# A two-layer decoder trunk on one core: half chunks of expert weights in a pinned order, and weights loaded as 8 KB runs

## The chip, the cores and the metric

The kernel runs on one core of a Trainium2 chip. The metric is the device time of one execution in microseconds; three runs of the kernel before took 2459.33, 2452.49 and 2456.84 us, median 2456.84. Engines are called PE (TensorE, with PEld for its weight loads), DVE (VectorE), ACT (ScalarE), POOL (GpSimd) and SP (SyncE). Each works through its own queue of instructions in order.

## The reference, cut to what matters

Two layers over 1024 tokens of width 1024, float32. Layer 0 mixes tokens with a convolution module, layer 1 with a gated linear recurrence (HGRN2); after each comes a mixture of experts, and at the end a norm. The change touches only the mixture of experts:

```python
def hier_moe(h, grp_w, grp_b, exp_w, exp_b, w_gate, w_up, w_down):
    ...
    gate = (grp_val * jax.nn.softmax(top_val, axis=-1)).reshape(-1)
    expert = (grp_idx * EXPERTS_PER_GROUP + top_idx).reshape(-1)
    ...
    def expert_block(args):
        xb, e = args
        return (jax.nn.silu(xb @ w_gate[e]) * (xb @ w_up[e])) @ w_down[e]

    y = lax.map(expert_block, (x_pad.reshape(n_blocks, MOE_BLOCK, D), block_expert)).reshape(n_rows, D)
    y = (y.astype(jnp.float32) * gate_pad[:, None]).astype(h.dtype)
    return jnp.zeros((T, D), h.dtype).at[tok_pad].add(y).reshape(B, S, D)
```

There are 32 experts with w_gate and w_up of 1024 x 512 and w_down of 512 x 1024; each token goes to two experts, and a block holds 128 rows of one expert.

## The kernel before

**The loop.** `moe(l, ...)` computes one block for each expert (32), and in layer 0 one more from a list of blocks beyond an expert's first 128 rows: 33 blocks in layer 0, 32 in layer 1 (a block of layer 1's list runs only where one is needed, behind the loop). A block's rows are gathered from HBM (`gather`, an indirect DMA on POOL, line 622, into `xg`), transposed on PE (`x_T`, 8 transposes of 128x128 into the PSUM tile `tp`, line 277) and written as two parts, `xh` by ACT (line 235) and `xl`, the rest, by DVE (line 236). Every float32 product is taken as three products of such parts: `xh wh`, `xh wl`, `xl wh`.

**The weights.** An expert's weights come in six chunks of 1 MB: two of gate, two of up, two of down, called `g0 g1 u0 u1 d0 d1` here. Each is a tile `wraw` of 128 partitions x 2048 words (`load_w`, one DMA on SP's queue, line 119). `moe_src` puts contraction row k * 128 + p on partition p, so that a chunk of gate or up has four runs of 2 KB per partition, and one of down two of 4 KB. `split` cuts a chunk into two halves of 128x1024 and makes `wh` (ACT, line 223) and `wl` (DVE, line 224) of each; four buffers (`WB`) hold each kind. Six products of 128x512 use one half: gate into `pg` and up into `pu` (lines 647 to 649), down into `pd` (lines 671 to 673). So a block has 12 halves, 72 products, and 8 + 4 transposes, four of them of the hidden rows `hh`.

**Behind the products.** ACT makes silu of `pg` (line 654), DVE multiplies it by `pu` into `hh` (line 655), PE transposes it (line 277), ACT and DVE write `hth` and `htl` (lines 235, 236), and the down products follow. ACT scales `pd` by the gate into `y` (line 677), and POOL scatters `y` to HBM (line 627).

**What sets the order.** The code writes for each block i: the gather for block i + 1, g0, the transposes of h of block i - 1, g1, x_T of block i + 1, u0, u1, silu and product, then d0 and d1 of block i - 1 and its y. That is only a start: a scheduler with a model of times places the instructions on each engine, so the order on an engine differs from block to block and from layer to layer. The loads have slots in a fixed turn: 14 chunks of layer 0 and 10 of layer 1 fit on chip, and are on their way before the loop begins; SP issues the next load when DVE has read the slot's last half. `PGB` = 1 gives one buffer each for `pg` and `pu` and two for `pd`.

**Two smaller parts** run inside the first blocks: `gate_table` (line 560 on) gives each row its gate, and `list_rest` and `entry` make the list of further blocks, on DVE and POOL above all, with small products on PE.

Of the kernel before, what the change touches and what calls it, by code (L numbers as in the profile page):

```python
# [7 lines left out]
F32 = mybir.dt.float32  # L8
# [36 lines left out]
EARLY = 3        # row tiles of h that are read back before the first MoE ends  # L45
# [34 lines left out]
CONV_DVE = (1, 2)   # the vector engine  # L80
CONV_PE = (4, 5, 6, 7)    # products
# [3 lines left out]
def trunk(ctx, tc, x, conv_norm_w, conv_pw1_w, conv_pw1_b, conv_dw_w, conv_dw_b, conv_ln_g, conv_ln_b,  # L85
# [29 lines left out]
    def load_w(ap3, pool=None):  # L115
        t = (pool or ring).tile([P, WIDE if pool is wides[0] else 2048], F32, name="wraw")[:, :2048]
        a, b = ap3.shape[1], ap3.shape[2]
        v = t.rearrange("p (a b) -> p a b", a=a)
        nc.sync.dma_start(v, ap3)
        return t  # L120
# [63 lines left out]
    def mixer_consts(t1, t2, t3, t4, lp):  # L184
        """what the recurrence needs of shapes and of its bounds; t1 and t2 hold 3 * 128, t3 and t4 224 words a row."""
# [6 lines left out]
        # softmax over the two layers, its cumulative sum less the first: the second one's share  # L192
# [23 lines left out]

    def split(pool, raw):
        """a chunk of weights, by halves, as its float32r part and what that leaves."""
        for i in range(2):
            hi = pool.tile([P, 1024], F32R, name="wh", bufs=WB)  # L220
            lo = pool.tile([P, 1024], F32R, name="wl", bufs=WB)
            r = raw[:, i * 1024:(i + 1) * 1024]
            nc.scalar.activation(hi, r, AF.Copy)  # L223
            nc.vector.tensor_tensor(lo, r, hi, op=OP.subtract)  # L224
            yield hi, lo
# [12 lines left out]
    def rsqrt_small(pool, v, n):  # L238
        """1/sqrt(v) for a few columns, on the vector engine alone: Newton steps, the scale left to the end."""
# [15 lines left out]
    def norm(pool, src, wbc, dst=None, scale=False):  # L255
        """rms norm of a [128, D] tile of rows."""
# [16 lines left out]
    def transpose_n(pp, src, c0, n=4, tag="tp"):  # L273
        """n [128,128] blocks of src from column block c0 on, transposed into one bank."""
        t = pp.tile([P, 512], F32, name=tag, **({"bufs": 2} if tag == "sc" else {}))
        for a in range(n):
            turned[0] = nc.tensor.transpose(t[:, a * P:(a + 1) * P], src[:, (c0 + a) * P:(c0 + a + 1) * P], ident)  # L277
        return t

    def rows_T(pp, src, hi, lo, cs, nb=KD, tag="tp"):  # L280
        """rows src [128, nb * 128] -> hi/lo [128, nb, cs] with columns on partitions."""
        for b in range(0, nb, 4):
            n = min(4, nb - b)
            t = transpose_n(pp, src, b, n, tag)[:, :n * P].rearrange("p (a c) -> p a c", a=n)
# [23 lines left out]
    def tail_b(pool, pp, router, l, j, res, r):  # L308
        """logits of a tile from its rows: the gain of the norm lies in the weights, its scale comes last."""
# [20 lines left out]
    def route(pool, router, i0, i1, ps):  # L330
        """the experts of the rows of tiles i0 to i1 - 1, their places among the experts' rows and what goes to these."""
# [8 lines left out]
        def first_max(v, w, mx, oh):  # L340
            """oh: one-hot of the first of the largest of v [P, n, w]; mx its value."""
# [25 lines left out]
        # rank: rows before it with the same expert, in these tiles and in the tiles done  # L367
# [9 lines left out]
        # the row of y that a place goes to less 8192, in two parts  # L377
# [20 lines left out]
        if i1 == NT:  # L398
# [3 lines left out]
            # empty places: 8192 + p, out of bounds  # L402
# [3 lines left out]
        else:  # L406
            # counts of up to 8 in each row
# [37 lines left out]
    def moe_blocks(l):  # L445
        """blocks in the order in which they are computed; NE is the first one of the list."""
        if not KEEPL[l]:
            return list(range(NE + LISTED[l]))
        return list(range(NE - 1)) + [NE] * LISTED[l] + [NE - 1]

    def moe_chunks(l):
        """(expert, part) in the order in which they are used."""
        seq, prev = [], None
        blocks = moe_blocks(l)
        for e in blocks:
# [22 lines left out]
    def moe(l, router, raws, slots, after, last=None):  # L478
        """all experts of a layer; slots are the pools of its weight chunks, in turn; after is called before the end.
        Where the last block's rows stay on chip, last is called with them in two parts."""  # L480
        with ExitStack() as held:
# [258 lines left out]
            for i, e in enumerate(blocks[:nb - (KEEPL[l])] + [None]):  # L740
# [10 lines left out]
                if i:  # L751
                    ht = h_T2(hs.pop(i - 1))
# [822 lines left out]
```

## Time and profile before

| | us |
|---|---|
| runs | 2459.33, 2452.49, 2456.84 (median 2456.84) |
| span of the profiled execution | 2454.5 |
| expert loop of layer 0, from its first gate product to the stretch's end | 478 to 1115 |
| expert loop of layer 1 | 1798 to 2409 |
| PE busy in these two | 608.20 of 637.00, 584.79 of 611.00 |
| granted clock in these two | 0.98, 0.99 |

The profiled execution is one run of the same program; its span lies between the fastest run and the median. In rows of the timeline, the bracket behind an instruction is the time for which its engine had stood idle before it, and what released it. An instruction's length on PE includes its way through the array: 128x512 products stand in the trace with 0.39 us each, while the next begins earlier. "x4" behind a row joins four equal instructions in a row.

### The profile page before, as it was taken

Reading aid. Unit: us, or ns where it says so; the run is one execution under the profiler, and the core shown is the slowest. Engines: PE = TensorE matmul, PEld = TensorE weight load, DVE = VectorE, ACT = ScalarE, POOL = GpSimd, SP = SyncE. Lnnn points to the kernel's source line nnn. Section 1 sums busy time; section 2 is a strip of 40 time slices with the busy share of each in tenths; the row PEclk is TensorE's granted clock in tenths of the full one; section 3 lists DMA queues with packets and bytes.
Section 4 is the critical chain, followed back from the end, with each engine's and each line's share of the span. In section 5 each row is a group of like instructions: output and inputs, shape, how many; then the busy total and the mean of one; then the engine's idle time right before and its main releaser. Section 6 shows DMA issues by size and latency. Waiting matters only on the chain. (4 is left out here: it accounts for less than half of the span.)

```text
span 2454.5 us, 31862 instructions
## 1 busy us (share of the span) xinstructions
PE 2237.0 (91%) x11755; PEld 1845.3 (75%) x11755; DVE 1861.1 (76%) x2525; ACT 1461.1 (60%) x2034; POOL 518.3 (21%) x331
## 2 busy tenths in 40 slices
PE   7998889699999989994799999989979999999997
PEld 6777767588887767773799999977758877777774
DVE  5999656599988778885377666673489988888887
ACT  5553145488887777784334334332358877777774
POOL 1998511311110111101100000020041111111103
PEclk9998989899999999996899999989989999999999
DMA  5111133699999999977402020106269999999985
GB/s 171 59 61 58 56 138 133 219 329 372 366 378 347 345 334 345 359 248 195 152 21 68 28 78 27 61 31 221 94 224 366 380 359 353 354 358 355 350 295 237
DMA packets 252857, 547.66 MB, mean 223 GB/s; under 512 B 27313, under 2 KB 60281, under 8 KB 252696
## 3 DMA queue, kind: packets, MB, share of 16 engines
q1 hardware_dynamic: 231412, 504.22, 58.7%
q0 software_dynamic: 18720, 33.60, 3.7%
q10 hardware_dynamic: 2564, 7.75, 0.9%
q8 instruction: 94, 1.54, 0.3%
q14 instruction: 67, 0.55, 0.1%
HBM read 519.66 MB, written 60.42 MB: 236 GB/s over the span
## 5 line engine op out<-in xcount | busy, mean ns | idle before, releaser
L224 DVE TENSOR_TENSOR wl<-wraw,wh 128x1024 fp32r<-128x1024 f32 x780 | 921.3, 1224 | 121.7 <-ACT wh L223 116.0
L223 ACT ACTIVATE wh<-wraw 128x1024 fp32r<-128x1024 f32 x780 | 795.8, 1059 | 126.3 <-PE pg L649 55.7
L647 PE MATMUL pg<-wh,xh 128*128 128x512 f32 x520 | 212.9, 409 | 17.6 <-ACT xh L235 16.8
L648 PE MATMUL pg<-wl,xh 128*128 128x512 f32 x520 | 213.3, 410 | 16.4 <-DVE wl L224 16.4
L649 PE MATMUL pg<-wh,xl 128*128 128x512 f32 x520 | 209.7, 403 | 5.6 <-DVE xl L236 5.6
L648 PE MATMUL pu<-wl,xh 128*128 128x512 f32 x520 | 206.5, 397 | 2.9 <-DVE wl L224 2.8
L672 PE MATMUL pd<-wl,hth 128*128 128x512 f32 x520 | 207.1, 398 | 2.1 <-DVE wl L224 1.7
L671 PE MATMUL pd<-wh,hth 128*128 128x512 f32 x520 | 206.4, 397 | 2.6 <-ACT wh L223 1.7
L647 PE MATMUL pu<-wh,xh 128*128 128x512 f32 x520 | 204.1, 393 | 0.0
L673 PE MATMUL pd<-wh,htl 128*128 128x512 f32 x520 | 204.1, 393 | 0.0
L649 PE MATMUL pu<-wh,xl 128*128 128x512 f32 x520 | 203.3, 391 | 0.0
L622 POOL DMA_INDIRECT xg<-xD,tidx x64 | 91.5, 1429 | 523.0 <-PE tp L277 470.8
L980 POOL TENSOR_TENSOR wraw<-wraw,tap 128x1024 f32<-128x1024 f32 x60 | 173.7, 2895 | 36.0 <-ACT tap L979 31.6
L627 POOL DMA_INDIRECT yD<-y,yidx x64 | 66.1, 1033 | 543.7 <-ACT y L677 538.1
L1247 PE MATMUL pa<-wih,xh 128*128 128x256 f32 x512 | 147.3, 288 | 2.6 <-ACT q L1228 2.6
L235 ACT ACTIVATE xh<-tp 128x512 fp32r<-128x512 f32 x146 | 84.4, 595 | 108.3 <-PE tp L277 107.6
L1247 PE MATMUL pa<-wil,xh 128*128 128x256 f32 x512 | 147.3, 288 | 0.0
L1247 PE MATMUL pa<-wih,xl 128*128 128x256 f32 x512 | 147.3, 288 | 0.0
L648 PEld LDWEIGHTS pg<-wl,xh 128*128 128x128 f32 x520 | 100.4, 193 | 48.7 <-DVE wl L224 29.6
L647 PEld LDWEIGHTS pg<-wh,xh 128*128 128x128 f32 x520 | 100.5, 193 | 41.6 <-ACT xh L235 19.4
L649 PEld LDWEIGHTS pg<-wh,xl 128*128 128x128 f32 x520 | 100.4, 193 | 30.7 <-DVE xl L236 11.1
L236 DVE TENSOR_TENSOR xl<-tp,xh 128x512 fp32r<-128x512 f32 x146 | 98.0, 685 | 31.1 <-ACT xh L235 29.7
(457 smaller groups left out, 4859.5 us busy)
## 6 DMA issues: line engine op xcount, KB each, us to landing
wraw<-in_moe_w_gate_dram SPq DMA_DIRECT2D x130, 1024.0 KB, 7.7
wraw<-in_moe_w_up_dram SPq DMA_DIRECT2D x130, 1024.0 KB, 7.9
wraw<-in_moe_w_down_dram SPq DMA_DIRECT2D x130, 1024.0 KB, 7.9
wraw<-in_hgrn_w_in_dram SPq DMA_DIRECT2D x16, 1024.0 KB, 8.1
wraw<-in_conv_pw_w_dram SPq DMA_DIRECT2D x12, 1024.0 KB, 9.8
xD<-xn SPq DMA_DIRECT2D x16, 512.0 KB, 2.9
my<-yD SPq DMA_DIRECT2D x16, 512.0 KB, 12.3
wraw<-yD SPq DMA_DIRECT2D x16, 512.0 KB, 9.8
```

Of the source, the lines that this page charges most:

```text
L223: nc.scalar.activation(hi, r, AF.Copy)
L224: nc.vector.tensor_tensor(lo, r, hi, op=OP.subtract)
L236: turned[2] = nc.vector.tensor_tensor(lo, ps, hi, op=OP.subtract)
L622: return nc.gpsimd.indirect_dma_start(out=xg, out_offset=None, in_=xD[l][:, :], in_offset=bass.IndirectOffsetOnAxis(ap=idx, axis=0), bound ...
L647: nc.tensor.matmul(ps, xh[:, kk], wh[:, k], start=(kk == 0), stop=False)
L648: nc.tensor.matmul(ps, xh[:, kk], wl[:, k], start=False, stop=False)
L649: done = nc.tensor.matmul(ps, xl[:, kk], wh[:, k], start=False, stop=(kk == KD - 1))
L671: nc.tensor.matmul(pd[:, ns], hh[:, kk], wh[:, ns], start=(kk == 0), stop=False)
L672: nc.tensor.matmul(pd[:, ns], hh[:, kk], wl[:, ns], start=False, stop=False)
L673: turned[0] = nc.tensor.matmul(pd[:, ns], hl[:, kk], wh[:, ns], start=False, stop=(kk == KF - 1))
L980: nc.gpsimd.tensor_tensor(res[c], res[c], t, op=OP.add)
L1247: nc.tensor.matmul(pa[:, :256], x_[:, k, js], w_[:, k].rearrange("p z c -> p (z c)"), start=(k == 0 and w_ is wh and x_ is xh), stop=(k == ...
```

## The change

It has three parts.

**Weights in one run per partition.** `moe_src` now puts contraction row p * 8 + k (p * 4 + k for down) on partition p, and a chunk is half of that partition's contiguous words: 2048 words, 8 KB, in one run. The contraction tile k of x then holds columns k, k + 8, k + 16 and so on, so `transpose_n` gets an argument `every` and reads `xg` with a stride of 8 words and `hh` with a stride of 4.

**An order written out.** `moe_halves` lists the half chunks in the order of use: g0, g1, u0, u1 of block i, then d0, d1 of block i - 1 (for the last block of layer 1 the down halves stand behind g0). The loop runs over halves; `s_` counts them in a block, 0 to 3 gate, 4 to 7 up, 8 to 11 down. `prepare(n + LEAD)` makes `wh` and `wl` of the half that is used three later. Around each group stands `with inorder`: every instruction of PE, DVE and ACT written in it gets a dependency, without a semaphore, on the one written before it on the same engine, so the scheduler keeps the order.

**Places.** x of block i + 1 is transposed behind the second and the third up half of block i; `hh` of block i is multiplied after the first down half of block i - 1; its transposes stand behind the third gate half of block i + 1; `y` of block i - 2 is made behind the first gate half of block i. The gather for block i + 2 is issued at the first gate half of block i, one block earlier than before.

Lines of the profile move with it: wh 223 becomes 222, wl 224 becomes 223, transposes 277 become 303, xh/hth and xl/htl 235 and 236 become 259 and 260, the gate and up products 647 to 649 become 682, the down products 671 to 673 become 710 to 712, silu 654 becomes 853 here, y 677 becomes 720.

On PE in layer 0, at the end of one block and the start of the next, before (pd is the down product, tp the transposes of the new block's x, pg the new block's gate):

```order
L673 MATMUL pd<-wh,htl 128x512
L277 MATMUL tp<-ident,xg_3529 128x128 x8
L647 MATMUL pg<-wh,xh 128x512
L648 MATMUL pg<-wl,xh 128x512
L649 MATMUL pg<-wh,xl 128x512
```

On PE in layer 1, before, where the up products end; hh is the hidden block that the up products have just completed, xg the rows of the next block:

```order
L649 MATMUL pu<-wh,xl 128x512
L671 MATMUL pd<-wh,hth 128x512
L277 MATMUL tp<-ident,hh 128x128 x4
L277 MATMUL tp<-ident,xg_15499 128x128 x4
L672 MATMUL pd<-wl,hth 128x512
L673 MATMUL pd<-wh,htl 128x512
```

On PE in layer 1, after, from the end of the second up half to the fourth (layer 0 has the same sequence):

```order
L682 MATMUL pu<-wh,xl 128x512
L303 MATMUL tp<-ident,xg_15500 128x128 x4
L682 MATMUL pu<-wh,xh 128x512
L682 MATMUL pu<-wl,xh 128x512
L682 MATMUL pu<-wh,xl 128x512
L682 MATMUL pu<-wh,xh 128x512
L682 MATMUL pu<-wl,xh 128x512
L682 MATMUL pu<-wh,xl 128x512
L303 MATMUL tp<-ident,xg_15500 128x128 x4
L682 MATMUL pu<-wh,xh 128x512
```

The next block's x is now transposed between up halves in both layers, six and five halves ahead of its first gate product, and no longer beside the transposes of hh.

On ACT in layer 1, before, one block's worth (xh and hth read the transposes, hh is silu, y reads pd):

```order
L223 ACTIVATE wh<-wraw 128x1024 x4
L654 ACTIVATE hh<-pg 128x512
L223 ACTIVATE wh<-wraw 128x1024 x4
L235 ACTIVATE xh<-tp 128x512
L223 ACTIVATE wh<-wraw 128x1024 x2
L235 ACTIVATE xh<-tp 128x512
L223 ACTIVATE wh<-wraw 128x1024 x2
L235 ACTIVATE hth<-tp 128x512
L677 ACTIVATE y<-pd,gates 128x1024
```

The same place after:

```order
L720 ACTIVATE y<-pd,gates 128x1024
L222 ACTIVATE wh<-wraw 128x1024 x2
L259 ACTIVATE hth<-tp 128x512
L222 ACTIVATE wh<-wraw 128x1024 x2
L853 ACTIVATE hh<-pg 128x512
L222 ACTIVATE wh<-wraw 128x1024
L259 ACTIVATE xh<-tp 128x512
L222 ACTIVATE wh<-wraw 128x1024
L259 ACTIVATE xh<-tp 128x512
L222 ACTIVATE wh<-wraw 128x1024 x6
```

Before, the first xh stands four wh's behind silu, and the two of a block lie on both sides of two wh's; after, the first stands one wh behind silu and the second one wh further, with six wh's ahead of the next y.

The diff, cut to its core:

```diff
+LEAD = 3
...
     def load_w(ap3, pool=None):
         t = (pool or ring).tile([P, WIDE if pool is wides[0] else 2048], F32, name="wraw")[:, :2048]
-        a, b = ap3.shape[1], ap3.shape[2]
-        v = t.rearrange("p (a b) -> p a b", a=a)
+        v = t if len(ap3.shape) == 2 else t.rearrange("p (a b) -> p a b", a=ap3.shape[1])
         nc.sync.dma_start(v, ap3)
         return t
...
+    class InOrder:
...
+        def __exit__(self, *_):
+            assert nc.cur_bb is self.at
+            for i in self.at.bb.instructions[self.n:]:
+                if i.engine in (ET.PE, ET.DVE, ET.Activation):
+                    if i.engine in self.last:
+                        tc.add_manual_dep(i, self.last[i.engine], mybir.DependencyInfo(
+                            mybir.DependencyClass.NoSync, mybir.DependencyReason.DATA), reason="in order")
+                    self.last[i.engine] = i.name
...
-    def transpose_n(pp, src, c0, n=4, tag="tp"):
+    def transpose_n(pp, src, c0, n=4, tag="tp", every=None):
         t = pp.tile([P, 512], F32, name=tag, **({"bufs": 2} if tag == "sc" else {}))
+        sv = src.rearrange("p (c k) -> p k c", k=every) if every else src.rearrange("p (k c) -> p k c", c=P)
         for a in range(n):
-            turned[0] = nc.tensor.transpose(t[:, a * P:(a + 1) * P], src[:, (c0 + a) * P:(c0 + a + 1) * P], ident)
+            turned[0] = nc.tensor.transpose(t[:, a * P:(a + 1) * P], sv[:, c0 + a], ident)
         return t
...
+    def moe_halves(l):
+        n, seq = len(moe_blocks(l)), []
+        def part(i, *chunks):
+            return [(i, p_, c, z) for p_, c in chunks for z in range(2)]
+        for i in range(n):
+            d = part(i - 1, ('d', 0), ('d', 1)) if i else []
+            if KEEPL[l] and i == n - 1:
+                seq += part(i, ('g', 0)) + d + part(i, ('g', 1), ('u', 0), ('u', 1))
+            else:
+                seq += part(i, ('g', 0), ('g', 1), ('u', 0), ('u', 1)) + d
+        return seq if KEEPL[l] else seq + part(n - 1, ('d', 0), ('d', 1))
...
     def moe_src(l, e, part, c):
+        w = {'g': moe_w_gate, 'u': moe_w_up, 'd': moe_w_down}[part]
+        cs = slice(c * 2048, (c + 1) * 2048)
...
-        if part == 'd':
-            return moe_w_down[l, e].rearrange("(k p) d -> p k d", p=P)[:, 2 * c:2 * c + 2, :]
-        w = moe_w_gate if part == 'g' else moe_w_up
-        return w[l, e].rearrange("(k p) f -> p k f", p=P)[:, 4 * c:4 * c + 4, :]
+        return w[l, e].rearrange("(p k) f -> p (k f)", p=P)[:, cs]
...
+            def prepare(n):
...
+                if z == 0:
+                    raw_of[key] = get(key)
+                with inorder:
+                    ready[n] = split_half(mp, raw_of[key], z)
...
+            for n, (i, part, c, z) in enumerate(seq):
+                prepare(n + LEAD)
+                e = blocks[i]
+                s_ = ('g', 'u', 'd').index(part) * 4 + 2 * c + z
+                with inorder:
+                    if part == 'g':
...
+                        done = mm_half(pgs[i], xt[i], ready.pop(n), 4 * c + 2 * z)
...
+                if s_ == 0:
+                    if i + 2 < nb:
+                        gather(xgs[i % 2], cols(blocks[i + 2])[0])
...
+                if s_ == 0 and i > 1 and i - 2 in pds:
+                    with inorder:
+                        finish(pds.pop(i - 2), cols(blocks[i - 2])[2], cols(blocks[i - 2])[1])
...
+                if s_ == (1 if KEEPL[l] and i == nb - 1 else 2) and i:
+                    turn_h(i - 1)
+                if s_ == 4:
+                    hs[i] = mp.tile([P, FE], F32, name="hlast" if KEEPL[l] and i == nb - 1 else "hh", bufs=HB)
+                    with inorder:
+                        nc.scalar.activation(hs[i], pgs.pop(i), AF.Silu)
+                if s_ in (5, 6) and i + 1 < nb:
+                    with inorder:
+                        xt[i + 1] = x_T(xgs[(i + 1) % 2], xt.get(i + 1), s_ - 5)
+                if s_ == 8 and i + 1 in pus:
+                    gate_h(i + 1)
```

More of the change, by code (lines that the diff above doesn't have):

```diff
@@ L215, in mixer_consts, with split_half, __init__, __enter__ @@
             nc.vector.tensor_tensor(msk[b], m2, m3, op=OP.mult)
+    def split_half(pool, raw, i):
+        hi = pool.tile([P, 1024], F32R, name="wh", bufs=WB)
+        lo = pool.tile([P, 1024], F32R, name="wl", bufs=WB)
+        r = raw[:, i * 1024:(i + 1) * 1024]
+        nc.scalar.activation(hi, r, AF.Copy)
+        nc.vector.tensor_tensor(lo, r, hi, op=OP.subtract)
+        return hi, lo
     def split(pool, raw):
         for i in range(2):
[L220 to L225, printed above, removed]
+            yield split_half(pool, raw, i)
+    class InOrder:
+        def __init__(self):
+            self.last = {}
+        def __enter__(self):
+            self.at = nc.cur_bb
+            self.n = len(self.at.bb.instructions)
+        def __exit__(self, *_):
[6 more added lines that the diff above has]
+                    self.last[i.engine] = i.name
     def split2(pool, raw, name, eng):
@@ L517, in rows_of @@
                 nc.vector.tensor_copy(yi, f[:, 3])
-            with tc.issue_after(listed):
-                for key in list(order)[:1]:
-                    early[key] = list(split(mp, early[key]))
             def sum3(dst, v, n, pool):
@@ L721, in cols @@
                 return first["e"][1][:, 0:1], first["e"][2][:, 0:1], first["e"][3][:, 0:1]
-            xt, hs = {}, {}
-            gather(xgs[0], cols(0)[0])
+            xt, hs, pgs, pus, pds = {}, {}, {}, {}, {}
+            inorder = InOrder()
+            seq = moe_halves(l)
+            raw_of, ready = {}, {}
+            def prepare(n):
+                if n >= len(seq):
+                    return
+                i, part, c, z = seq[n]
+                key = (blocks[i], part, c)
+                if KEEPL[l] and i == nb - 1 and key not in order_last:
+                    for k_, at in zip([(key[0], p_, c_) for p_ in 'gud' for c_ in range(2)], LSLOT[l]):
+                        order[k_] = at
+                        order_last[k_] = early[k_] = get(k_)
+                if z == 0:
+                    raw_of[key] = get(key)
+                with inorder:
+                    ready[n] = split_half(mp, raw_of[key], z)
+            order_last = {}
+            with tc.issue_after(listed):
+                for n in range(LEAD - 1):
+                    prepare(n)
+            g0 = gather(xgs[0], cols(0)[0])
             g1 = gather(xgs[1], cols(1)[0])
-            xt[0] = x_T(xgs[0])
+            with inorder:
+                xt[0] = x_T(xgs[0])
+            prepare(LEAD - 1)
             if KEEPL[l]:
@@ new lines, in turn_h, with gate_h @@
+            def turn_h(i):
+                with inorder:
+                    hs[i] = h_T2(hs[i])
+            def gate_h(i):
+                with inorder:
+                    nc.vector.tensor_tensor(hs[i], pus.pop(i), hs[i], op=OP.mult)
+            for n, (i, part, c, z) in enumerate(seq):
[5 more added lines that the diff above has]
+                        if s_ == 0:
+                            pgs[i] = pp.tile([P, FE], F32, name="pg", bufs=PGB)
+                        done = mm_half(pgs[i], xt[i], ready.pop(n), 4 * c + 2 * z)
+                    elif part == 'u':
+                        if s_ == 4:
+                            pus[i] = pp.tile([P, FE], F32, name="pu", bufs=PGB)
+                        mm_half(pus[i], xt[i], ready.pop(n), 4 * c + 2 * z)
+                    else:
+                        if s_ == 8:
+                            pds[i] = pp.tile([P, D], F32, name="pd", bufs=3 - PGB)
+                        mm_down_half(pds[i], hs[i], ready.pop(n), 2 * c + z)
+                if s_ == 0:
+                    if i + 2 < nb:
+                        gather(xgs[i % 2], cols(blocks[i + 2])[0])
+                    if i and i - 1 in pus:
+                        gate_h(i - 1)
+                if s_ == 0 and i > 1 and i - 2 in pds:
+                    with inorder:
+                        finish(pds.pop(i - 2), cols(blocks[i - 2])[2], cols(blocks[i - 2])[1])
+                if i == 0 and s_ == 1:
+                    with tc.issue_after(g1.ins):
+                        gate_table(done.ins)
+                    rp.release()
+                    rp = apool(f"rest{l}", 1)
+                if s_ == (1 if KEEPL[l] and i == nb - 1 else 2) and i:
+                    turn_h(i - 1)
+                if s_ == 4:
+                    hs[i] = mp.tile([P, FE], F32, name="hlast" if KEEPL[l] and i == nb - 1 else "hh", bufs=HB)
+                    with inorder:
+                        nc.scalar.activation(hs[i], pgs.pop(i), AF.Silu)
+                if s_ in (5, 6) and i + 1 < nb:
+                    with inorder:
+                        xt[i + 1] = x_T(xgs[(i + 1) % 2], xt.get(i + 1), s_ - 5)
+                if s_ == 8 and i + 1 in pus:
+                    gate_h(i + 1)
+                    if i + 1 == nb - 1:
+                        last_turn = n + 2
+                if KEEPL[l] and s_ == 11 and i == nb - 2:
+                    with inorder:
+                        finish(pds.pop(i), cols(blocks[i])[2], cols(blocks[i])[1])
+                if not KEEPL[l] and s_ == 11 and i == nb - 2:
+                    turn_h(nb - 1)
+                if s_ == 11 or (i == 0 and s_ == 7):
+                    i += s_ == 11
@@ L778, in moe @@
                 e = blocks[-1]
-                keys = [(e, part, c) for part in 'gud' for c in range(2)]
-                for key, pool in zip(keys, LSLOT[l]):
-                    order[key] = pool
-                    early[key] = get(key)
-                pg = pp.tile([P, FE], F32, name="pg", bufs=PGB)
-                pu = pp.tile([P, FE], F32, name="pu", bufs=PGB)
-                for c in range(2):
-                    mm_in(pg, xt[nb - 1], get((e, 'g', c)), c)
-                for c in range(2):
-                    mm_in(pu, xt[nb - 1], get((e, 'u', c)), c)
-                hlast = h_T(pg, pu, "hlast")
+                gate_h(nb - 1)
+                hlast = hs[nb - 1]
+            else:
+                for i in (nb - 2, nb - 1):
+                    if i in pds:
+                        with inorder:
+                            finish(pds.pop(i), cols(blocks[i])[2], cols(blocks[i])[1])
             left = after()
```

92 lines of the change are left out of this document (34 added, 58 removed).

## The prediction

> **What bounds the kernel now.** I read the page's engine rows first, then busy time in stretches, then the timeline and the waits inside the slow ones. The page gives the span; the runs shown (2452.49 to 2459.33) have their median 2.3 us above it, so I sum against 2454.5 and add 2.3 at the end.
>
> ```profile
> span 2454.5 us, 31862 instructions
> PE 2237.0 (91%) x11755; PEld 1845.3 (75%) x11755; DVE 1861.1 (76%) x2525; ACT 1461.1 (60%) x2034; POOL 518.3 (21%) x331
> ```
>
> The expert loops fill 478 to 1115 us (33 blocks) and 1798 to 2409 us (32 blocks). Busy time in stretches, each cut into an early and a late part, and then two stretches inside the second loop; the columns are length, then PE, weight load, DVE, ACT, POOL with their counts, the granted clock, the DMA share and GB/s:
>
> ```profile
> 478.00:728.00 250.00, 249.12 (x1189) 201.09 (x1188) 234.94 (x316) 210.74 (x236) 50.39 (x52) 0.99 0.98 347
> 728.00:1115.00 387.00, 359.09 (x1620) 288.34 (x1618) 318.40 (x306) 293.01 (x325) 42.60 (x36) 0.98 0.91 323
> 1798.00:1979.00 181.00, 177.92 (x850) 147.00 (x849) 163.86 (x198) 147.41 (x166) 41.06 (x48) 0.98 0.95 345
> 1979.00:2409.00 430.00, 406.87 (x1833) 317.96 (x1830) 358.37 (x349) 324.48 (x371) 48.27 (x42) 1.00 0.94 338
> 1871.00:1942.00 71.00, 71.00 (x340) 59.12 (x338) 66.22 (x66) 61.61 (x69) 8.31 (x8) 1.00 1.02 378
> ```
>
> The same view of the transposes (line 277) alone:
>
> ```profile
> 728.00:1115.00 387.00, 30.98 (x223) 26.94 (x221) 0.98 0.91 323
> 1979.00:2409.00 430.00, 34.31 (x248) 28.52 (x246) 1.00 0.94 338
> 1871.00:1942.00 71.00, 6.70 (x52) 5.88 (x50) 1.00 1.02 378
> ```
>
> The early parts have a full PE (4 us idle in 431), the late parts don't. For the floor I need the pace of back-to-back work. A stretch of the timeline in layer 0 (start, length, engine, line, what, and in brackets the idle time before and its releaser), with one row of layer 1 behind it:
>
> ```profile
> 888.83 0.39 PE L672 MATMUL pd<-wl,hth 128*128 128x512 f32 x1
> ...
> 891.10 0.39 PE L673 MATMUL pd<-wh,htl 128*128 128x512 f32 x1
> ...
> 891.33 1.03 PE L277 MATMUL tp<-ident,xg 128*128 128x128 f32 x8
> 891.53 1.11 ACT L677 ACTIVATE y<-pd,gates 128x1024 f32<-128x1024 f32 x1 [0.30 <-PE pd L673]
> 892.54 1.05 ACT L223 ACTIVATE wh<-wraw 128x1024 fp32r<-128x1024 f32 x1
> ...
> 893.48 1.07 ACT L235 ACTIVATE xh<-tp 128x512 fp32r<-128x512 f32 x2
> 893.62 1.22 DVE L224 TENSOR_TENSOR wl<-wraw,wh 128x1024 fp32r<-128x1024 f32 x1 [1.14 <-ACT wh L223]
> ...
> 894.12 0.50 PE L647 MATMUL pg<-wh,xh 128*128 128x512 f32 x1 [1.76 <-ACT xh L235]
> ...
> 895.50 0.50 PE L649 MATMUL pg<-wh,xl 128*128 128x512 f32 x1 [0.64 <-DVE xl L236]
> ```
>
> ```profile
> 1888.66 0.60 PE L277 MATMUL tp<-ident,xg 128*128 128x128 f32 x4
> ```
>
> From 888.83 to 891.10 are ten products: 0.227 us each. Eight transposes take 1.03 and four 0.60, so one more costs 0.1075. A block has 72 products and 12 transposes: 72 x 0.227 + 12 x 0.1075 = **17.63 us**. Check on the stretch at 1871: 288 x 0.227 + 52 x 0.1075 = 71.0, what it took. So four blocks in a row already run at the floor, with DVE busy 66.22 and ACT 61.61 of 71: the same work fits beside PE when its order is right.
>
> The late parts against that floor: layer 0, 1397 x 0.227 + 223 x 0.1075 = 341.1 of 387, 45.9 over; layer 1, 1585 x 0.227 + 248 x 0.1075 = 386.5 of 430, 43.5 over. Together **89.4 us over 2982 / 72 = 41.4 blocks**, about 2.2 a block.
>
> What holds PE there? In layer 0 the timeline above says it: the block's own x is transposed right ahead of its gate products, and on ACT the copy of y and a wh stand ahead of xh. PE is 1.76 + 0.64 us without work and loses its overlap twice. In layer 1 it is again ACT's place in the queue:
>
> ```profile
> 2261.47 3.90 ACT L223 ACTIVATE wh<-wraw 128x1024 fp32r<-128x1024 f32 x4
> ...
> 2267.41 0.66 PE L277 MATMUL tp<-ident,hh 128*128 128x128 f32 x4 [0.56 <-DVE hh L655]
> 2267.90 0.60 PE L277 MATMUL tp<-ident,xg 128*128 128x128 f32 x4
> ...
> 2268.54 0.60 ACT L235 ACTIVATE xh<-tp 128x512 fp32r<-128x512 f32 x1 [3.17 <-PE tp L277]
> 2269.03 2.00 ACT L223 ACTIVATE wh<-wraw 128x1024 fp32r<-128x1024 f32 x2
> ```
>
> ACT stands 3.17 us at xh with four wh's done and others queued behind it; xg's transposes stand behind hh's, and those wait for DVE. The bill comes later, where PE lacks a wl. The waits of layer 1 from 2057 to 2372 (16 blocks), then one of layer 0 from 728 to 1115 (total, times, longest):
>
> ```profile
> ACT xh L235 <- PE tp L277: 53.7, 24, 3.6
> PEld pg L648 <- DVE wl L224: 18.7, 24, 1.1
> PE pg L648 <- DVE wl L224: 9.9, 16, 0.7
> ```
>
> ```profile
> PEld pg L647 <- ACT xh L235: 18.9, 9, 2.9
> ```
>
> It is not the transfers. Over 2000 to 2370 DVE waited for a load once, and over the whole span SP, which issues them, waited for slots that DVE had not yet emptied:
>
> ```profile
> DVE wl L224 <- DMA wraw<-in_moe_w_up_dram: 0.3, 1, 0.3
> ```
>
> ```profile
> SPq L119 <- DVE wl L224: 943.7, 335, 12.8
> ```
>
> **The change, part by part.** *The order.* Nothing is added on PE, ACT or DVE; instructions change places, and the ties hold each engine to its own order, without a semaphore. A half chunk is six products, 1.36 us. From gate half 0 at time 0: h's transposes stand at 4.1, the up halves begin at 5.9, x's transposes of the next block stand at 8.6 and 10.4, the down halves begin at 12.2, the next block at 17.63. So xh and xl are made 6 to 9 us before their gate products, instead of right ahead: the stalls of both layers above have no cause left. What is late next? wh for half n+3 can start when PE leaves half n-1: release 0.30 (y's row above), from wh's start to wl's 893.62 - 892.54 = 1.08, wl 1.22: 2.6 us after half n begins. PE needs that wl at 3 x 1.36 + 0.23 = 4.3. The margin of 1.7 covers the longest piece put between, y with 1.11 on ACT; behind y stand two wh's, and PE waits for those, so y is the nearest thing to a new stall, with 0.6 left. xh may stop ACT for about 0.7 us, until its transposes end, with the wh of a down half behind it: covered too. hh stands behind the wl of the last down half, so it finds pu complete; h's transposes come seven halves after pu's end. Finding PE idle there would cost what it finds now, at most 18.7 / 16 = 1.2 us a block by the row of PEld pg; the fast stretch says 0.
>
> *DVE and ACT as bounds*: 66.22 / 4 = 16.6 and 61.61 / 4 = 15.4 us a block in the fast stretch, under 17.63. DVE has 1 us to spare, no more.
>
> *The transposes read with a stride* (32 bytes in x, 16 in h). Line 1121 does the like with 8 words of stride in this trace; its weight loads (min/median/max), and four of its transposes:
>
> ```profile
> L1121 PEld LDWEIGHTS tp<-ident,wraw x32: 185/193/227, 302.3 to 418.5; 128*128 128x128 f32 x32
> ```
>
> ```profile
> 351.59 0.61 PE L1121 MATMUL tp<-ident,wraw 128*128 128x128 f32 x4
> ```
>
> Four take 0.61 against 0.60 at line 277. The weight load of a plain one is 28.52 us / 246 = 0.116 with its overlaps; if 0.193 were not hidden, 12 x (0.193 - 0.116) = 0.9 us a block. Bounds 0 and 0.9; the row of four is the nearest, so nearly nothing. I put 0.2 a block for this and the margins together: 41.4 x 0.2 = 8.3.
>
> The Trainium skill speaks against this edit: "SBUF — State Buffer", section "Door 1: The DMA port swizzle (why `[64,N]` ≈ `[32,N]`)", says that accesses pay a penalty for each new 16-byte line, so fp32 strides are free only up to 4 words. By that x's 8 transposes would pay and h's 4 not: an estimate of 8 x 0.077 x 65 = 40 us, 2412. The longer load of line 1121 agrees; its four transposes in 0.61 us say that the load stays hidden.
>
> *The loads.* The page and three stretches of DMA rows (packets, MB, share of 16 engines): 1871 to 1942, the 1 KB runs of a weight load at 1290 to 1300, and reads of y from HBM at 1120 to 1140.
>
> ```profile
> wraw<-in_moe_w_down_dram SPq DMA_DIRECT2D x130, 1024.0 KB, 7.9
> ```
>
> ```profile
> q0 software_dynamic: 18720, 33.60, 3.7%
> ```
>
> ```profile
> q1 hardware_dynamic: 10598, 25.12, 95.6%
> q0 software_dynamic: 1152, 1.66, 6.3%
> ```
>
> ```profile
> q1 hardware_dynamic: 1040, 1.05, 36.4%
> ```
>
> ```profile
> q1 hardware_dynamic: 1163, 4.27, 90.0%
> ```
>
> A block loads six chunks, 6.29 MB, and gathers and scatters 33.60 / 65 = 0.52: 6.81 MB, 18.0 us at the 378 GB/s seen. That is 0.2 to 0.4 over the pace, but by the kernel's slots 14 chunks of layer 0 and 10 of layer 1 are on chip when the loop starts (2.33 and 1.67 blocks), so transfers bind only from 33 x 17.83 / 30.7 = 19.2 us a block in layer 0 and 32 x 17.83 / 30.3 = 18.8 in layer 1. Now 8 KB runs: the mix of 2 and 4 KB took 0.956 x 16 x 71 / 10598 = 102.5 ns per 2370 B, the 1 KB runs 0.364 x 160 / 1040 = 56 ns per 1008 B. A line through both gives 301 ns for 8 KB, the mix's own rate 354 ns. With 768 packets a block on 16 engines, and 1.1 us for queue 0, that is 15.6 to 18.1 us. Under 18.8: no cost, and no gain beyond the slack, as PE never waited for a load. These are estimates; no row has 8 KB runs of weights.
>
> *Sum.* 89.4 of excess go, 8.3 come, and I keep 4 in layer 0 for its clock of 0.98 (2% of 387 is 7.7, half of it where PE stood idle anyway): 2454.5 - 89.4 + 8.3 + 4 = 2377.4, **2380 us** with the 2.3. The unknown margins alone give 2371 (none) to 2421 (1.2 a block).
>
> **The rivals.** *Each block keeps about a microsecond* (y or a strided load on PE's path, or DVE's 1 us used up by small waits): 41.4 x 1.0 in place of 8.3 gives 2413. For: DVE at 93% in the fast stretch. Against: that stretch lost nothing. Loads at 19.5 us a block (384 ns a run) come to the same: 30.7 x 19.5 - 588 = 11 and 30.3 x 19.5 - 571 = 20, so 2411. Chance 0.17.
>
> *More goes*: 637 + 611 - 65 x 17.63 = 102 lie over the floor in all, 13 outside the late parts. Without them, the 8.3 and the 4: 2454.5 - 102 + 2.3 = 2355. Chance 0.08; list and gate work on DVE remains, which speaks against.
>
> *It changes nothing*: 2457, chance 0.03, if something else than the order placed the transposes; the order rows speak against it.
>
> *Slower: 8 KB runs, one per partition at 16 KB pitch, read like y's rows.* Those rows of 4 KB lie 512 KB apart and took 0.900 x 320 / 1163 = 248 ns per 3671 B. At that rate 8 KB takes 553 ns and a block 27.6 us: 30.7 x 27.6 + 30.3 x 27.6 - 1248 = 436, so 2892. The loops become longer than today from 20.7 and 20.1 us a block, about 400 ns a run. Against: 16 KB is far from 512, and the slots' lead pays part. Chance 0.09.
>
> The Trainium skill has a rule on this ("DMA: Bandwidth & Descriptors", section "Latency and other measured facts"): a pitch of 512 KiB between partitions' rows gives 207 GB/s, larger powers of two less. The reads of y agree (4.27 MB in 20 us is 214 GB/s); no run here shows 16 KB pitch with 8 KB runs.
>
> **How the numbers follow.** The forecast has 0.63, the rivals 0.17, 0.08, 0.03 and 0.09. A measurement of this kernel tells about 0.3% from no change, 7.4 us. Faster 0.63 + 0.17 + 0.08 = 0.88, same 0.03, slower 0.09. The range runs from the case in which more goes to just past the margins' upper bound: 2355 to 2425.
>
> **What would show it.** Right: both loops at 17.6 to 18.0 us a block, PE busy over 98% in the late parts too, no row of PE behind ACT xh, ACT's wait at xh under 1 us. The loads are right if DVE has no wait for wraw and a run takes 300 to 350 ns. It is wrong if PE shows waits for wl in the half after y (margin), if four transposes take over 0.8 us (stride), if the granted clock falls where PE is full, or if DVE waits for loads from the third block on.

## The result and the profile after

The changed kernel takes **2379.34 us** (median of four runs, 2379.11 to 2380.95) against 2456.64 (2452.49 to 2459.33): a ratio of 0.9687, interval 0.9676 to 0.9699, 77 us faster. The page after, with the two groups that make the split weights:

```profile
span 2377.3 us, 31779 instructions
PE 2209.9 (93%) x11755; PEld 1856.7 (78%) x11755; DVE 1868.6 (79%) x2525; ACT 1461.4 (61%) x2034; POOL 546.4 (23%) x331
...
L223 DVE TENSOR_TENSOR wl<-wraw,wh 128x1024 fp32r<-128x1024 f32 x780 | 929.0, 1226 | 74.7 <-ACT wh L222 63.6
L222 ACT ACTIVATE wh<-wraw 128x1024 fp32r<-128x1024 f32 x780 | 805.0, 1057 | 87.6 <-PE pd L712 59.3
```

The counts are those of before, and so is the length of one instruction; what shrank is the idle time (121.7 and 126.3 before). Busy time in four stretches of the changed kernel (columns as in the prediction: length, PE, weight load, DVE, ACT, POOL, clock, DMA share, GB/s), then the transposes of line 303 alone in the second and fourth:

```profile
478.00:728.00 250.00, 248.16 (x1179) 201.79 (x1178) 237.32 (x316) 208.82 (x235) 61.01 (x49) 1.00 0.95 350
728.00:1050.00 322.00, 322.00 (x1522) 269.81 (x1521) 301.17 (x291) 273.86 (x308) 44.02 (x34) 1.00 0.98 381
1755.00:1979.00 224.00, 220.50 (x1050) 182.35 (x1050) 209.90 (x237) 186.19 (x209) 54.31 (x50) 1.00 0.96 357
1979.00:2308.00 329.00, 329.00 (x1556) 275.67 (x1555) 307.89 (x298) 279.77 (x315) 46.10 (x35) 1.00 0.98 380
```

```profile
728.00:1050.00 322.00, 33.16 (x216) 33.13 (x216) 1.00 0.98 381
1979.00:2308.00 329.00, 33.88 (x222) 33.73 (x220) 1.00 0.98 380
```

In both late parts PE is busy without a gap. At the prediction's paces (0.227 us a product, 0.1075 a transpose) the second stretch should take 1306 x 0.227 + 216 x 0.1075 = 319.7 us and took 322; the fourth 1334 x 0.227 + 222 x 0.1075 = 326.7 and took 329. So 0.13 us a block remain over the floor, where before 2.2 did. The period can be read off the transposes of h in two blocks that follow each other (timeline of PE):

```profile
911.72 0.63 PE L303 MATMUL tp<-ident,hh 128*128 128x128 f32 x4
...
929.50 0.63 PE L303 MATMUL tp<-ident,hh 128*128 128x128 f32 x4
```

That is 17.78 us, and by the first gate products blocks 11 to 31 of layer 0 and 4 to 30 of layer 1 all have it. The longest waits of DVE and of ACT (728 to 1050; total, times, longest) and ACT's order within one block:

```profile
DVE wl L223 <- ACT wh L222: 17.6, 36, 0.7
ACT xh L259 <- PE tp L303: 16.7, 36, 0.6
```

```profile
908.80 1.10 ACT L720 ACTIVATE y<-pd,gates 128x1024 f32<-128x1024 f32 x1
909.80 2.00 ACT L222 ACTIVATE wh<-wraw 128x1024 fp32r<-128x1024 f32 x2
...
916.96 0.60 ACT L259 ACTIVATE xh<-tp 128x512 fp32r<-128x512 f32 x1 [0.64 <-PE tp L303]
```

ACT still stops at xh, but 0.6 us at most, in layer 1 (1979 to 2308) too, where it was 3.6 there before. In the whole list PE appears only as what is waited for.

Where the 77 us lie, by the first gate product of a block in the two timelines (us):

| piece | before | after |
|---|---|---|
| start to layer 0's first gate product | 478.2 | 476.6 |
| layer 0, blocks 0 to 13 | 249.9 | 253.2 |
| layer 0, blocks 14 to 31 | 362.6 | 320.0 |
| layer 0's block 32 and the whole HGRN stage | 707.8 | 705.0 |
| layer 1, blocks 0 to 7 | 143.6 | 143.8 |
| layer 1, blocks 8 to 29 | 429.6 | 391.2 |
| layer 1, blocks 30 and 31, and the end | 82.7 | 87.5 |

The late blocks give 42.6 + 38.4 = 81.0. Two pieces got clearly longer: the early blocks of layer 0 by 3.3 and the end by 4.8. Two got shorter, by 1.6 and 2.8; the change barely touches them, and the first of them varies from 473.7 to 479.3 in the traces of the other runs. The end has this on ACT (the last row's idle time is the point) and this on PE:

```profile
2308.82 1.10 ACT L720 ACTIVATE y<-pd,gates 128x1024 f32<-128x1024 f32 x1
...
2313.03 1.06 ACT L222 ACTIVATE wh<-wraw 128x1024 fp32r<-128x1024 f32 x1 [3.10 <-SPq L895]
```

```profile
2314.62 0.80 PE L710 MATMUL pd<-wh,hth 128*128 128x512 f32 x1 [3.61 <-ACT hth L259]
```

### The profile page after: what moved, and what is told of

Same layout as the page of the kernel before. It is cut to its first block, busy times and chain, and to the rows that moved or that the text cites. A ratio compares the mean times of both kernels' runs of the same rounds, so it can differ in the third digit from the quotient of the medians.

```text
span 2377.3 us, 31779 instructions
## 1 busy us (share of the span) xinstructions
PE 2209.9 (93%) x11755; PEld 1856.7 (78%) x11755; DVE 1868.6 (79%) x2525; ACT 1461.4 (61%) x2034; POOL 546.4 (23%) x331
## 5 line engine op out<-in xcount | busy, mean ns | idle before, releaser
L222 ACT ACTIVATE wh<-wraw 128x1024 fp32r<-128x1024 f32 x780 | 805.0, 1057 | 87.6 <-PE pd L712 59.3
L682 PE MATMUL pu<-wh,xh 128*128 128x512 f32 x520 | 213.6, 411 | 0.0
L682 PE MATMUL pg<-wl,xh 128*128 128x512 f32 x520 | 205.0, 394 | 0.1
L682 PE MATMUL pg<-wh,xl 128*128 128x512 f32 x520 | 204.1, 392 | 0.0
L661 POOL DMA_INDIRECT yD<-y,yidx x64 | 81.7, 1277 | 519.1 <-ACT y L720 511.7
L710 PEld LDWEIGHTS pd<-wh,hth 128*128 128x128 f32 x520 | 98.6, 190 | 27.1 <-ACT hth L259 4.7
L711 PEld LDWEIGHTS pd<-wl,hth 128*128 128x128 f32 x520 | 98.4, 189 | 23.5 <-DVE wl L223 3.2
L1078 ACT ACTIVATE tap<-upl,dwT 128x1024 f32<-128x1024 f32 x60 | 68.9, 1150 | 77.5 <-POOL wraw L1079 77.5
L712 PEld LDWEIGHTS pd<-wh,htl 128*128 128x128 f32 x520 | 98.6, 190 | 21.6 <-DVE htl L260 1.3
```

The source lines that it names most:

```text
L661: s = nc.gpsimd.indirect_dma_start(out=yD[l][:, :], out_offset=bass.IndirectOffsetOnAxis(ap=idx, axis=0), in_=y, in_offset=None, bounds_ch ...
L682: done = nc.tensor.matmul(ps, x_[:, kk + k], w_[:, k], start=(kk + k == 0 and x_ is xh and w_ is wh), stop=(kk + k == KD - 1 and x_ is xl))
L710: nc.tensor.matmul(pd[:, ns], hh[:, kk], wh[:, ns], start=(kk == 0), stop=False)
L711: nc.tensor.matmul(pd[:, ns], hh[:, kk], wl[:, ns], start=False, stop=False)
L712: turned[0] = nc.tensor.matmul(pd[:, ns], hl[:, kk], wh[:, ns], start=False, stop=(kk == KF - 1))
L1078: nc.scalar.activation(t, src, AF.Copy, scale=dwT[:, c, lag:lag + 1])
```

## The experiments

All times are medians; a run with a single time is named so. The kernel before, run beside them, had 2455.0 to 2456.0.

### The two halves of the change apart

**The order alone.** The changed kernel with the old reading of the weights and plain transposes; PE, ACT and DVE keep the changed kernel's sequence.

```diff
-        return w[l, e].rearrange("(p k) f -> p (k f)", p=P)[:, cs]
+        return w[l, e].rearrange("(k p) f -> p k f", p=P)[:, 4 * c:4 * c + 4, :]
...
-                    t = transpose_n(pp, xg, 4 * b, every=KD).rearrange("p (a c) -> p a c", a=4)
+                    t = transpose_n(pp, xg, 4 * b).rearrange("p (a c) -> p a c", a=4)
```

> The pinned order with the weights loaded as before (runs of 2 and 4 KB, transposes without a stride); PE, ACT and DVE have the same instructions in the same order as the changed kernel. Theory (the order does all of it, transfers and strides cost nothing that shows): 2370 to 2380 us, a block in the middle of a loop at 17.63 to 17.78 us. Rival (the 8 KB runs are needed, because PE now asks for 6.81 MB per 17.78 us, 383 GB/s, and 2 and 4 KB runs gave 378 at most): the lead of 14 and 10 chunks is used up within a loop, DVE waits for loads towards its end, 2385 to 2420 us.

Measured: 2388.78 us (ratio to before 0.9736, 0.972 to 0.9752). Neither theory had it right. The blocks take 17.77 us to the end of both loops, as the theory says; yet it is 9.4 us slower than the changed kernel, inside the rival's range. The two profiled executions are 11.3 us apart, and 7.5 of these lie at the end (95.0 us from block 30's first gate product, where the changed kernel has 87.5): in the last block ACT waits as in the changed kernel, only longer:

```profile
2324.07 1.06 ACT L222 ACTIVATE wh<-wraw 128x1024 fp32r<-128x1024 f32 x1 [10.37 <-SPq L897]
```

**The layout alone.** The kernel before with the new `moe_src` and the strided transposes; the scheduler's sequence on PE, ACT and DVE stayed that of before.

> The scheduler's order of before with the weights loaded as 8 KB runs and the transposes read with a stride; PE, ACT and DVE have the same instructions in the same order as the kernel before. Theory (layout alone is worth nothing): within 0.3% of before, 2450 to 2464 us, PE's waits behind ACT xh and DVE wl as before. Rival (shorter transfers free slots earlier and let wh and wl run ahead): at least 10 us faster. Other rival (the strided loads cost on PE's path, 0.6 to 0.9 us a block): 2490 or more.

Measured: 2459.88 us, ratio 1.0028 (1.0018 to 1.0038): the theory. If anything it is 0.3% slower. The wait that carried the prediction is still there (2057 to 2372, 53.7 before):

```profile
ACT xh L234 <- PE tp L278: 54.1, 24, 3.7
```

**The ties.** The same written order, without the dependencies:

```diff
                 if i.engine in (ET.PE, ET.DVE, ET.Activation):
-                    if i.engine in self.last:
+                    if False:
```

> The changed kernel written in the same order, without the ties that hold PE, ACT and DVE to it: the scheduler places the instructions. Theory (it was the scheduler's order on the in-order engines that cost, and the writing alone doesn't cure it): most of the gain goes, 2420 to 2470 us. Rival (the half chunks, the longer lead of the weights and the earlier gather are the gain, ties or not): within 5 us of 2379.

Measured: 2456.47 us, ratio 1.0005 (0.999 to 1.002). The whole gain is gone: half chunks, the longer lead and the earlier gather bring nothing as long as the scheduler places the instructions. The old waits come back, in layer 1 (2050 to 2350) and in layer 0, where before had 1.76:

```profile
ACT xh L259 <- PE tp L303: 50.2, 22, 3.7
```

```profile
896.12 0.50 PE L682 MATMUL pg<-wh,xh 128*128 128x512 f32 x1 [1.75 <-ACT xh L259]
```

**Ties on ACT alone** (`if i.engine == ET.Activation`).

> The changed kernel with ties on ACT alone; the scheduler places PE's and DVE's instructions. ACT's order is nearly the changed kernel's, PE has x's transposes among the down products again. Theory (ACT's place for xh helps only if PE's transposes stand ahead of it too): ACT waits at xh for PE's transposes with wh's queued behind, most of the 77 us stays lost, 2410 to 2470 us. Rival (ACT's order alone is the cure): 2379 to 2395.

Measured, one run: 2436.8 us, so three quarters of the gain stay lost. ACT's order by itself doesn't help layer 0 (blocks 14 to 31 take 363.4 us, 362.6 before), where PE's transposes stand among the down products again and ACT waits for them (800 to 1000):

```profile
ACT xh L259 <- PE tp L303: 46.9, 10, 4.7
```

Blocks take 20.1 us there and 18.3 in layer 1. So layer 1 is another matter: the scheduler places x's transposes behind the first gate product and among the up products, ACT's wait at xh is gone from the list (2057 to 2340; 53.7 us from 2057 to 2372 before), and blocks 8 to 29 take 404.3 us, which is 25 of the 38 us gained there. Ties on PE or on DVE alone were not run.

### Which place in the order

**The lead.** `LEAD = 2`.

> The changed kernel with LEAD = 2: each wh and wl stands one half chunk (1.36 us) later in the queues of ACT and DVE. Theory (the margin at LEAD = 3 is 1.7 us, with y's 1.11 between 0.6): at 2 the wh behind y, behind hth and behind xh come too late, 0.5 to 1.5 us of PE idle a block, 2410 to 2475 us, with PE rows waiting for DVE wl. Rival (the four buffers set the lead, the place in the queue does not matter): 2379 to 2385.

Measured, one run: 2415.45 us, the theory's lower end; blocks of 18.37 us, 0.59 more. PE's weight loads wait for wl again (800 to 1000):

```profile
PEld pd L711 <- DVE wl L223: 6.5, 22, 0.4
```

That is two waits a block, at the second and the fourth down half; a third stands at the second up half (3.7 us in all, before overlap). In the block traced they come where DVE has htl, xl or hh among its wl's, and none comes in the gate halves behind y.

**x's transposes late.**

```diff
-                if s_ in (5, 6) and i + 1 < nb:
+                if s_ in (5, 6) and i == 0:
...
+                if s_ == 11 and i + 2 < nb:
+                    with inorder:
+                        xt[i + 2] = x_T(xgs[i % 2])
```

> The changed kernel with both groups of x's transposes of the next block placed behind the last down half, right ahead of the block's own gate products, where layer 0 of the kernel before had them. Everything else stays pinned. Theory (the late place of x is what stalled layer 0): PE waits for ACT xh, 0.9 us at least (release 0.3 and one xh of 0.6), up to the 2.4 us seen there, for 63 blocks: 2435 to 2530 us. Rival (the kernel before lost its time to the order of wh and wl, and x's place is nearly free): under 2400.

Measured, one run: 2426.54 us, 18.55 us a block: between the two, 0.77 a block where 0.9 was the least expected. The late place alone is not the 2.4 us that layer 0 had lost. PE's own idle time before the first gate product is 0.2 us a block (800 to 1000); the rest shows as weight loads that wait for xh and xl:

```profile
PEld pg L682 <- ACT xh L259: 4.7, 11, 0.4
PEld pg L682 <- DVE xl L260: 4.7, 11, 0.4
PE pg L682 <- ACT xh L259: 2.6, 11, 0.2
```

**And y ahead of it on ACT**: the run before with `finish` of the same block written ahead of `x_T`.

> The run with x's transposes behind the last down half (2426.5 us, 18.55 us a block), and the block's own y now ahead of xh on ACT, as layer 0 of the kernel before had it (there with a wh between, too). Theory (what ACT has ahead of xh is what makes the late place dear): y adds its 1.11 us to PE's wait, 19.4 to 20.2 us a block, 2475 to 2530 us. Rival (ACT has slack, y there costs nothing): 2420 to 2435.

Measured, one run: 2461.92 us, 19.11 us a block; below the range, but the direction is the theory's. y costs 0.56 a block, half its length, and that is what PE's idle time grows by; where the other half is covered was not traced. PE's idle time ahead of the first gate product is 0.8 us a block now (same window):

```profile
PEld pg L682 <- ACT xh L259: 10.9, 11, 1.0
...
PE pg L682 <- ACT xh L259: 8.8, 11, 0.8
```

These two places, wrong together, cost 82.6 us: a pinned order can be as slow as the scheduler's. It is not the same loss, though. The late blocks of the profiled execution take 343.9 and 420.3 us, so 53 of the 81.0 us come back there, and some 25 are lost in the early blocks of both layers, where the kernel before had lost little.

### The stride

> The changed kernel with x and hh transposed without a stride, so that rows of x and hh meet other rows of the weights than they should; loads, order and counts are those of the changed kernel. It prices the stride alone. A block of the changed kernel takes 17.78 us where 72 products and 12 transposes at the paces of before come to 17.63. If the stride is the 0.15: 17.63 a block, 65 x 0.15 = 10 us less, 2370. If the 0.15 is something else (the joints between products and transposes): 2379 as it is.

The edit is the second pair of lines of the first diff, and the like for `hh`. Measured: 2378.84 us (2377.32 to 2380.09): it is not the stride. The weight loads of x's transposes fall back from 191 to 140 ns (median) and those of hh from 205 to 139, and a block takes 17.77 us for 17.78. The changed kernel's two rows come first, then two of this run:

```profile
L303 PEld LDWEIGHTS tp<-ident,xg x520: 185/191/230, 474.8 to 2300.6; 128*128 128x128 f32 x174
L303 PEld LDWEIGHTS tp<-ident,hh x256: 197/205/212, 497.7 to 2310.6; 128*128 128x128 f32 x128
```

```profile
L303 PEld LDWEIGHTS tp<-ident,xg x520: 138/140/231, 477.5 to 2300.0; 128*128 128x128 f32 x174
L303 PEld LDWEIGHTS tp<-ident,hh x256: 138/139/144, 499.1 to 2310.0; 128*128 128x128 f32 x128
```

```profile
912.72 0.60 PE L303 MATMUL tp<-ident,hh 128*128 128x128 f32 x4
...
930.49 0.60 PE L303 MATMUL tp<-ident,hh 128*128 128x128 f32 x4
```

The joints between products and transposes remain as the explanation of the 0.15; no run takes them apart.

### The loads

**What transfers can do**, with wl left out of the expert blocks so that they are the bound; first 8 KB runs, then 2 and 4 KB.

> Transfers made the bound: the changed kernel (8 KB runs) without wl in the expert blocks, so without the third product of each three; PE has 48 products and 12 transposes a block, 12.2 us, ACT some 14.5, and the loads 6.81 MB. What the transfers can do shows in the time of a block. Theory (8 KB runs take 301 to 354 ns each, as a line through the shorter runs gave): 15.6 to 18.1 us a block once the lead is used up, 376 to 437 GB/s, with engines waiting for loads. Rival (a run of 8 KB takes 400 ns or more): over 20 us a block.

> The same without wl, with the old layout (runs of 2 and 4 KB). Theory (the mix moves 23.1 bytes per ns and engine, as in the kernel before): 17.7 to 18.3 us a block, 372 to 385 GB/s, slower than the 8 KB runs by 0 to 2.5 us a block. Rival (the layout makes no difference to what the transfers can do): the same time a block within 0.1 us.

Measured, one run each: 2296.20 and 2357.99 us. Busy time from 750 to 950, q1's packets there (q1 is the queue of the weight loads) and what ACT waits for, the 8 KB kernel first:

```profile
750.00:950.00 200.00, 161.47 (x694) 112.64 (x694) 30.09 (x45) 169.34 (x197) 23.12 (x23) 1.00 1.00 402
```

```profile
q1 hardware_dynamic: 9949, 72.45, 90.0%
```

```profile
ACT wh L787 <- DMA wraw<-in_moe_w_gate_dram: 23.1, 20, 1.4
```

```profile
750.00:950.00 200.00, 160.44 (x658) 109.37 (x659) 29.40 (x44) 162.41 (x187) 22.13 (x22) 0.97 1.02 382
```

```profile
q1 hardware_dynamic: 28857, 68.49, 91.8%
```

By the first gate products, blocks 14 to 29 of layer 0 take 17.5 and 18.3 us; both theories hold, the second at the end of its range, and both rivals fall. Per engine the 8 KB runs move 72.45 MB / (0.900 x 16 x 200 us) = 25.2 bytes per ns, the others 23.3. So the layout is worth 5% of the transfers' rate, and PE's 17.78 lies between the two: 8 KB runs keep ahead of it, 2 and 4 KB runs fall behind.

**The last loads.** `prepare` fetches all six chunks of block 31 at once, and by the program's order SP issues its d1 between g0 and d0 of block 30, and block 30's own d1 last of all, into the slot that g0 of block 31 leaves. SP's issues in the changed kernel:

```profile
2280.82 3.76 SPq L119 DMA_DIRECT2D wraw<-in_moe_w_down_dram  x2
2295.51 0.33 SPq L119 DMA_DIRECT2D wraw<-in_moe_w_gate_dram  x1
2298.60 3.75 SPq L119 DMA_DIRECT2D wraw<-in_moe_w_up_dram  x2
2305.01 3.20 SPq L119 DMA_DIRECT2D wraw<-in_moe_w_down_dram  x2
```

The second of the pair at 2305.01 is the load that ACT's wh at 2313.03 waits for. The edit, on the changed kernel and on the order with the old layout:

```diff
                         order_last[k_] = early[k_] = get(k_)
+                        if k_ == key:
+                            for dk in [(blocks[i - 1], 'd', c_) for c_ in range(2)]:
+                                raw_of[dk] = get(dk)
-                if z == 0:
+                if z == 0 and key not in raw_of:
```

> The changed kernel with one thing moved: the two down chunks of block 30 of layer 1 are issued ahead of the chunks g1, u0, u1, d0, d1 of block 31, not behind them, so that they take slots that are free earlier; the last down chunk of block 31 takes the late slot instead. In the changed kernel ACT waits 3.10 us for the last of these loads and PE stands 3.9 us. Theory (that wait is the slot's lateness): the wait goes, 3 to 4 us less, 2375 to 2377 us. Rival (the late slot only moves the wait to block 31's own down chunk, behind the branch): 2379 or a little more.

> The pinned order with the old layout of the weights (runs of 2 and 4 KB) and the same move of block 30's down chunks. There ACT waits 10.37 us for the last load of block 30, and the kernel takes 2388.8 us. Theory (transfers in 2 and 4 KB runs keep the queue full, 1.02 of its time, and run behind by the loop's end; the layout's 9 us are nearly all in this one wait): the wait goes, 2379 to 2382 us, within 5 us of the same move on the changed kernel. Rival (the old layout costs in the loops or elsewhere): 2385 or more.

Measured: **2373.13** us (2371.42 to 2375.94; ratio to before 0.9665, 0.9648 to 0.9681) and 2373.47 (2370.04 to 2375.03; 0.966, 0.9644 to 0.9676). The wait is gone; ACT's row after y in the first of them:

```profile
2307.96 1.10 ACT L720 ACTIVATE y<-pd,gates 128x1024 f32<-128x1024 f32 x1
2308.96 1.05 ACT L222 ACTIVATE wh<-wraw 128x1024 fp32r<-128x1024 f32 x1
```

The gain is 6.2 us where 3 to 4 were expected; the last stretch, 87.5 us long, now takes 82.4. PE's wait explains 2.9 of these 5.1: it was 3.61 us and is 0.69. Most of the rest is the clock: after the wait the changed kernel's products start 0.43 us apart and not 0.227, and the granted clock (third number from the end) is 0.51 over the 5.4 us that follow.

```profile
2314.60:2320.00 5.40, 5.23 (x12) 3.66 (x13) 3.28 (x4) 1.97 (x2) 0.00 (x0) 0.51 0.03 8
```

```profile
2317.01 0.63 PE L711 MATMUL pd<-wl,hth 128*128 128x512 f32 x1
2317.44 0.63 PE L712 MATMUL pd<-wh,htl 128*128 128x512 f32 x1
```

Block 30's 24 down products take 8.35 us there from the first start to the next gate product, and 6.20 with the edit, where the clock stays at 1.00 (2309 to 2317). On the old layout the gain is 15.3 us, 12.6 of them in the last block (22.8 us from its first gate product to the first of its second gate chunk, with block 30's down products between; 10.2 now); the rest was not traced. With this wait out of the way **the two layouts take the same time**. The old one is close to the edge, though: in block 29 of layer 1 it begins to wait for loads (ACT's timeline of that run).

```profile
2287.81 2.01 ACT L222 ACTIVATE wh<-wraw 128x1024 fp32r<-128x1024 f32 x2 [0.93 <-DMA wraw<-in_moe_w_gate_dram]
```

## Why the prediction was right, point by point

**The bound and the excess.** The floor of 17.63 us a block and the 89.4 us above it were right: the same blocks now run at 0.13 over it. Without the ties nothing is left of it.

**The cause.** ACT's queue, in both layers, held as a mechanism: putting x's transposes and y back where layer 0 had them brings back 53 of the 81 us in the late blocks. But it was told too simply. The late x alone costs 0.77 us a block, y ahead of it 0.56 more; 1.33 of layer 0's 2.4. About 0.35 more is the clock (next but one paragraph). The rest may come from the order of wh, wl and y around it, which was not taken apart further. And ACT's order alone cures two thirds of layer 1 and nothing of layer 0: there PE's and ACT's must fit. For layer 1 the evidence is that run and the wait at xh that comes and goes with the loss; x's place there was not moved by itself.

**The margins.** The walk gave 1.7 us at a lead of three halves and 0.6 with y between. At three, no block of the late parts waits, so 0.6 was enough. A lead of two, 1.36 less, costs 0.59 a block, near the -0.7 that the walk would then give, but that is partly luck: the walk puts the first stall behind y, and the run has none there. The wl's that come late stand where DVE has xl, htl or hh between, which the walk did not follow.

**The terms that were off.** 0.2 a block was kept and 0.13 came; 4 us were kept for the clock of 0.98 in layer 0, and it is 1.00 now. The clock was not a price that stays: in the trace of before it fell to half four times in layer 0's late blocks, 17 us in all by the trace's clock records, each time right behind waits of PE, here one of 2.71 us.

```profile
828.41 0.50 PE L647 MATMUL pg<-wh,xh 128*128 128x512 f32 x1 [2.71 <-ACT xh L235]
```

```profile
829.00:834.00 5.00, 4.17 (x13) 3.17 (x13) 2.34 (x4) 1.06 (x1) 0.10 (x1) 0.66 1.04 404
```

Products started 0.43 us apart there, some 6 us lost over 18 blocks, and this went together with the waits. The late blocks therefore gave 81.0 us, 4 more than the 77.1 of the sum. Two terms were missing that make up for it: the early blocks of layer 0, 3.3 us longer (the tie-less run has 250.3 us there and the changed kernel 253.2, so the ties seem to cost it, beside the work on the list), and the end, 4.8 longer; 4.4 us came back in the two pieces that the change barely touches. That the sum hit 2380 by 0.7 us owes something to this: it is luck that these cancel.

**The step that failed** is "Under 18.8: no cost" for the loads. It was true for the loops, and the rate was sized rightly (15.6 to 18.1 us a block, 17.5 measured). But it looked at the mean demand alone, and not at the order in which SP issues the last six chunks: there one load comes late, and PE pays, 3.61 us of wait and about 2 more at half the clock behind it. Following SP's queue to its last rows would have found it.

**The rivals.** Slow reads at a pitch of 16 KB are refuted: 402 GB/s. The stride that the Trainium skill warns of ("SBUF — State Buffer", section "Door 1: The DMA port swizzle (why `[64,N]` ≈ `[32,N]`)") shows in the weight load, 191 for 140 ns, and not in the time: 2379.3 with it and 2378.8 without. By the prediction's reading of it hh's stride of 4 words would cost nothing; hh's loads take 205 ns for 139.

## What to carry to other kernels

When PE's work per block is known and some blocks already run at that pace, the excess of the others is the gain to expect from an order; and an order that is only written, not tied, may bring none of it. Such an order has to be checked on all queues that feed it, in its last block too: the one load that came late cost 6 us here, and 15 with the shorter runs. A wait of PE can cost more than its length, because the products behind it may run at half the clock. After such a gain look at the next bound: here PE's 17.78 us a block stand 0.3 above what 8 KB loads can do, and already under what 2 and 4 KB loads can.

## What the runs showed of the hardware that was not expected

With the DMA engines full, weight loads in runs of 8 KB, with the gathers and scatters beside them, moved 397 to 402 GB/s on one core, and those in runs of 2 and 4 KB 378 to 382. The Trainium skill ("DMA: Bandwidth & Descriptors", section "Where 436 GB/s comes from") puts the limit of HBM at about 358 GB/s per core, which is a stack's 716 GB/s divided by its two cores. This kernel runs on one core, and that half did not bind it: the 8 KB runs are 11 to 12% above it, the shorter ones 6 to 7%.

PE's granted clock fell behind waits as short as those of this kernel. After PE's wait of 3.61 us the granted clock was 0.51 over the next 5.4 us; after one of 0.69 us it stayed at 1.00. In layer 0's late blocks of before both waits of 2.71 us were followed by a half clock of 3.4 or 6.8 us, and of six waits of 1.76 us two.
